# Routing with 112 candidate sums, VectorE in the written order, and placing from an earlier pair on

## The chip, the cores and the metric

The kernel runs on one core of a Trainium2 chip. The metric is the device time of one execution in microseconds (us). Five engines run side by side, each through its own list of instructions in order: TensorE (PE, with its weight loads as PEld), VectorE (DVE), ScalarE (ACT), GpSimd (POOL) and SyncE (SP, which starts the DMAs). An instruction that waits for another engine holds up everything behind it on its own engine.

## The reference, cut to what matters

Two transformer blocks follow each other on 256 tokens of width 1024. The change lies in the feed-forward part at the end of the first block, which looks up single-neuron experts by product keys:

```python
s = jnp.einsum('nhpd,hpkd->nhpk', qry, sub_keys)          # 256 tokens, 8 heads, 2 halves, 128 keys
s_top, i_top = lax.top_k(s, 16)
cand = (s_top[:, :, 0, :, None] + s_top[:, :, 1, None, :]).reshape(n, 8, 16 * 16)
sc, ci = lax.top_k(cand, 16)
e_a = jnp.take_along_axis(i_top[:, :, 0], ci // 16, axis=-1)
e_b = jnp.take_along_axis(i_top[:, :, 1], ci % 16, axis=-1)
experts, gw = e_a * 128 + e_b, jax.nn.softmax(sc, axis=-1)
act = gelu(einsum('td,tkd->tk', xb, u_tab[experts]))       # u_tab, v_tab: 16384 x 1024
out = einsum('tk,tkd->td', gw * act, v_tab[experts])
```

Each token and head takes the 16 best keys of either half, forms 16 x 16 sums of two scores, and keeps the 16 best of these. Since both lists are sorted, the sum of ranks a and b (counted from 0) has at least (a+1)(b+1)-1 sums that are no smaller.

## The kernel before, in words

The kernel does not gather. It multiplies all 16384 rows of `peer_u` with all tokens: 128 blocks of 128 experts, taken two at a time in 64 pairs (`u_pair`, called by `pre`). A pair loads 1 MB of `peer_u` (three buffers, `raw`), which is cut into four pieces of 128x512, called splits here and numbered s0, s1, ... over all pairs, so that pair n has the splits 4n to 4n+3. `split` makes two tiles of each: ACT rounds it to `wh` (L132), and POOL or DVE forms the remainder `wl` (L127); both have four buffers. PE then runs 12 matmuls for each split, 48 for a pair, the third of them being the first that needs `wl`. A gelu on ACT follows (L1074). So the cast of split s has to wait until PE has finished split s-4, whose buffer it takes.

Which engine makes a `wl` goes by a turning pattern, `lo_pat`: while the routing is computed it is `"pppppv"`, five on POOL and the sixth on DVE; while the experts are placed it is `"vp"`.

Routing (`route(t)`, for the two halves t = 0, 1 of the tokens) is DVE work. Per half it runs `top16` (L1110 to L1115) on 16 rows of 128 scores, forms 8 x 256 candidate sums (L1131), runs `top16` on the 8 rows of 256, and turns the found places into expert numbers by comparing, multiplying and adding up over 128x2048 elements (L1149 to L1152, twice). A `top16` is five instructions, each of which needs the one before: the 8 largest (L1111), their places (L1112), their replacement by a very small number (L1113), the next 8 largest (L1114) and their places (L1115). In the profile L1112, L1113 and L1115 are two instructions each, a load of the 8 values (MATCH_VALUE_LOAD) and the search. ACT takes the exponentials of the weights (L1156). PE then transposes the three results `ee` (L1164), and ACT and DVE bring them into `eab` and `gwb` (L1166 to L1172). `route` is a generator: between its pieces the loop calls `pre`, 26 times in all, so the pairs and the routing are written into each other.

Placing follows: for each of 32 groups of eight tokens DVE builds one-hot rows (`onehots`, four instructions of 128x1024), PE multiplies them (L1210, 16 matmuls) and the result, the weights at their experts' places, is multiplied into what `pre` left (`place`). The groups are spread over the pairs from the end of routing up to pair 62.

The order of the instructions on each engine is not the written one: a scheduler sets it when the kernel is built, by its own costs and priorities. It also moves the transposes and the exponential among the pairs.

Of the kernel before, what the change touches and what calls it, by code (L numbers as in the profile page):

```python
# [8 lines left out]
F32 = mybir.dt.float32  # L9
F32R = mybir.dt.float32r  # L10
BF = mybir.dt.bfloat16
HF = mybir.dt.float16
# [7 lines left out]
EPS = 1e-6  # L20
AHEAD = 3
GSC = 16384.0
NEG = -3.0e38
TAKEN = -3.39e38
TAKEN_LIM = -3.2e38
# [29 lines left out]
def block_kernel(ctx, tc, I, out, dbg=None, stop=None):  # L55
# [978 lines left out]
    with ExitStack() as pp:  # L1034
# [42 lines left out]
                V.tensor_tensor(a[:, :, 0:t], pv[:, :, 0:t], a[:, :, 0:t], op=ALU.mult)  # L1077

        npre = 0
        with ExitStack() as pr:  # L1080
            R = pr.enter_context(tc.tile_pool(name="R", bufs=2))
            iota = R.tile([128, 128], F32, name="iota", bufs=1)
# [31 lines left out]
                V.max(vals[:, 8:16], src)  # L1114
                V.max_index(idxs[:, 8:16], vals[:, 8:16], src)  # L1115

            def route(t):
                val = R.tile([128, 16, 16], F32, name="val")
                idx = R.tile([128, 16, 16], U32, name="idx")
                for hp in range(16):  # L1120
                    top16(sc_[t][:, hp * 128:hp * 128 + 128], val[:, hp], idx[:, hp])
                    if hp % 4 == 3:
                        yield
                idf = R.tile([128, 16, 16], HF, name="idf")
                V.tensor_copy(idf, idx)
                cand = z0[:, 4096:6144].rearrange("p (h a b) -> p h a b", h=8, a=16)
                eq = R.tile([128, 8, 16, 16], HF, name="eq", bufs=1)
                vv = val.rearrange("p (h two) k -> p h two k", two=2)
                iv = idf.rearrange("p (h two) k -> p h two k", two=2)
                B4 = [128, 8, 16, 16]  # L1130
                V.tensor_tensor(cand, vv[:, :, 0, :, None].to_broadcast(B4),  # L1131
                                vv[:, :, 1, None, :].to_broadcast(B4), op=ALU.add)
                yield
                top = R.tile([128, 8, 16], F32, name="top")
                ci = R.tile([128, 8, 16], U32, name="ci")
                for hh in range(8):
                    top16(cand[:, hh].rearrange("p a b -> p (a b)"), top[:, hh], ci[:, hh])
                    if hh % 2:
                        yield
                ee = R.tile([128, 3, 128], F32, name="ee")  # L1140
                for w in range(2):
                    cu = R.tile([128, 8, 16], U32, name="cu", bufs=1)
                    if w == 0:
                        V.tensor_single_scalar(cu, ci, 4, op=ALU.logical_shift_right)
                    else:
                        V.tensor_single_scalar(cu, ci, 15, op=ALU.bitwise_and)
                    cf_ = R.tile([128, 8, 16], HF, name="cf", bufs=1)
                    V.tensor_copy(cf_, cu)
                    V.tensor_tensor(eq, cf_[:, :, :, None].to_broadcast(B4),  # L1149
                                    iob[:, None, None].to_broadcast(B4), op=ALU.is_equal)  # L1150
                    V.tensor_tensor(eq, eq, iv[:, :, w, None, :].to_broadcast(B4), op=ALU.mult)
                    V.tensor_reduce(ee[:, w].rearrange("p (h k) -> p h k", h=8), eq, axis=AX.X, op=ALU.add)  # L1152
                    yield
                gw = ee[:, 2].rearrange("p (h k) -> p h k", h=8)
                V.tensor_tensor(gw, top, top[:, :, 0:1].to_broadcast([128, 8, 16]), op=ALU.subtract)
                S.activation(gw, gw, AF.Exp)  # L1156
                gs = R.tile([128, 8], F32, name="gs")
                V.tensor_reduce(gs, gw, axis=AX.X, op=ALU.add)
                V.reciprocal(gs, gs)
                V.tensor_tensor(gw, gw, gs[:, :, None].to_broadcast([128, 8, 16]), op=ALU.mult)  # L1160
                yield
# [5 lines left out]
                gr = R.tile([128, 128], F32, name="gr", bufs=1)  # L1167
                S.mul(gr, q[:, 256:384], GSC)
                for i in range(2):
                    V.tensor_copy(gwb[:, i, ts], gr)  # L1170
                    if i < 1:
                        V.tensor_tensor(gr, gr, gwb[:, i, ts], op=ALU.subtract)  # L1172
                yield

            for g in range(4):
                add(f"pq{g}", I["w_peer_q"][g], "f", pair(xt), qry(g))
            need("pq3")
            lo_pat[0] = "pppppv"
            for t in range(2):
                for _ in route(t):  # L1180
                    pre(npre)
                    npre += 1

        lo_pat[0] = "vp"
        zone["ze"] = Zt("ze").rearrange("p (b t) -> p b t", t=256)
        with ExitStack() as pe:
# [35 lines left out]
            hot = onehots(0)  # L1222
            for n in range(n0, 64):
                pre(n)
                while ng < 32 and ng * (n1 - n0) < 32 * (n + 1 - n0):
# [568 lines left out]
```

## Time and profile before

| | us |
|---|---|
| median of 3 runs (lowest to highest) | 1726.85 (1726.26 to 1728.38) |
| the profiled execution | 1726.9 |
| its span in the profile | 1725.1 |
| PE busy | 1686.9 (98%) |
| DVE busy | 1248.7 (72%) |
| ACT busy | 989.8 (57%) |
| POOL busy | 247.4 (14%) |

The profiled execution stands within 0.1 us of the median of the runs, and 1.8 us of it lie outside the span. The pairs run from about 583 to 1001 us of the span; the routing on DVE lies between 545 and 668 us. The last column but two of a row by stretches of time (PEclk) is the clock granted to PE as a share of its full 2.4 GHz.

### The profile page before, as it was taken

The page shows a single profiled execution, that of the slowest core. Times are in us where ns is not written, and L with a number is a line of the kernel's source. Part 1 is how long each engine was busy: PE and PEld are TensorE (multiplying, and loading weights), DVE is VectorE, ACT ScalarE, POOL GpSimd, SP SyncE. Part 2 cuts the span into 40 slices and gives each one's busy share as a digit, 9 for nine tenths or more (in the row PEclk, how much of TensorE's full clock was granted, in tenths as well). Part 3 has the DMA queues.
Part 4 walks back from the last instruction along what each step waited for, and adds up shares of the span by engine and source line. Part 5 has one row for each costly group of instructions (what it writes and reads, how often), then busy time and mean ns, then how long its engine had stood idle before and what let it go on. Part 6 is the DMA issues. An engine that isn't in the chain of part 4 may idle for free.

```text
span 1725.1 us, 30196 instructions
## 1 busy us (share of the span) xinstructions
PE 1686.9 (98%) x11502; PEld 1523.2 (88%) x11502; DVE 1248.7 (72%) x2517; ACT 989.8 (57%) x1984; POOL 247.4 (14%) x182
## 2 busy tenths in 40 slices
PE   9999999999999988999999999999999899999997
PEld 7988978998989988999999988878888796889996
DVE  7956999557667995066888856656666679688887
ACT  7565687556555544555555555545555663666664
POOL 0000000000000477754444400000000000000001
PEclk9999999999999999999999999999999999999998
DMA  6448424555445444544445465575555547345552
GB/s 249 157 165 291 171 91 137 191 199 186 151 142 202 160 147 147 195 171 149 167 151 172 147 205 192 193 281 194 193 194 195 210 172 306 128 177 196 175 193 98
DMA packets 45746, 312.22 MB, mean 181 GB/s; under 512 B 5536, under 2 KB 6048, under 8 KB 8992
## 3 DMA queue, kind: packets, MB, share of 16 engines
q1 hardware_dynamic: 45600, 310.29, 51.5%
q8 instruction: 90, 1.47, 0.3%
q14 instruction: 56, 0.46, 0.1%
HBM read 307.65 MB, written 2.62 MB: 180 GB/s over the span
## 4 chain that ended last, share of the span: by engine, by line
PE 90%; DVE 6%; ACT 2%; DMA 1%; issue 1%; POOL 1%; SPq 0%; POOLq 0%; ACTq 0%
PE y L1258 7%; PE y L1257 7%; PE pm L1065 7%; PE y L1259 7%; PE pm L1067 6%; PE pm L1066 6%; PE pm L204 6%; PE pm L206 6%; PE pm L205 6%; PE pm L197 4%; PE pm L198 4%; PE pm L196 4%; PE pt L204 2%; PE pt L206 2%; PE pt L205 2%; PE pt L1210 2%
## 5 line engine op out<-in xcount | busy, mean ns | idle before, releaser
L132 ACT CAST wh<-raw 128x512 fp32r<-128x512 f32 (+1 forms) x1048 | 643.7, 621 | 555.1 <-PE pm L1066 172.6
L127 DVE TENSOR_TENSOR wl<-raw,wh 128x512 fp32r<-128x512 f32 (+1 forms) x886 | 607.6, 692 | 328.1 <-ACT wh L132 326.1
L1067 PE MATMUL pm<-xhi,wl 128*128 128x256 f32 x1024 | 292.3, 285 | 8.4 <-POOL wl L127 4.9
L1065 PE MATMUL pm<-xhi,wh 128*128 128x256 f32 x1024 | 294.4, 288 | 0.0
L1066 PE MATMUL pm<-xlo,wh 128*128 128x256 f32 x1024 | 291.6, 285 | 0.0
L127 POOL TENSOR_TENSOR wl<-raw,wh 128x512 fp32r<-128x512 f32 x162 | 229.9, 1423 | 250.9 <-ACT wh L132 246.8
L1067 PEld LDWEIGHTS pm<-xhi,wl 128*128 128x128 f32 x1024 | 198.2, 194 | 9.7 <-POOL wl L127 5.5
L1066 PEld LDWEIGHTS pm<-xlo,wh 128*128 128x128 f32 x1024 | 198.6, 194 | 0.0
L1065 PEld LDWEIGHTS pm<-xhi,wh 128*128 128x128 f32 x1024 | 198.1, 193 | 0.0
L204 PE MATMUL pm<-xhi,wh 128*128 128x256 f32 x640 | 182.6, 286 | 1.0 <-ACT wh L132 1.0
L206 PE MATMUL pm<-xhi,wl 128*128 128x256 f32 x640 | 180.9, 284 | 1.0 <-DVE wl L127 1.0
L205 PE MATMUL pm<-xlo,wh 128*128 128x256 f32 x640 | 181.1, 283 | 0.5 <-DVE xlo L309 0.5
L204 PEld LDWEIGHTS pm<-xhi,wh 128*128 128x128 f32 x640 | 122.4, 192 | 6.0 <-issue 3.4
L206 PEld LDWEIGHTS pm<-xhi,wl 128*128 128x128 f32 x640 | 122.3, 192 | 2.3 <-DVE wl L127 1.4
L205 PEld LDWEIGHTS pm<-xlo,wh 128*128 128x128 f32 x640 | 122.6, 192 | 1.7 <-issue 0.8
L204 PE MATMUL pt<-xhi,wh 128*128 128x256 f32 x320 | 90.9, 284 | 0.0
L206 PE MATMUL pt<-xhi,wl 128*128 128x256 f32 x320 | 90.5, 283 | 0.0
L205 PE MATMUL pt<-xlo,wh 128*128 128x256 f32 x320 | 90.5, 283 | 0.0
L197 PE MATMUL pm<-wl,xhi 128*128 128x512 f32 (+1 forms) x192 | 76.1, 396 | 0.1
L196 PE MATMUL pm<-wh,xhi 128*128 128x512 f32 (+1 forms) x192 | 74.7, 403 | 1.4 <-ACT wh L132 1.2
L198 PE MATMUL pm<-wh,xlo 128*128 128x512 f32 (+1 forms) x192 | 74.4, 390 | 0.0
L204 PEld LDWEIGHTS pt<-xhi,wh 128*128 128x128 f32 x320 | 61.3, 192 | 0.9 <-ACT ua L1628 0.4
(1057 smaller groups left out, 3576.2 us busy)
## 6 DMA issues: line engine op xcount, KB each, us to landing
raw<-peer_u SPq DMA_DIRECT2D x64, 1024.0 KB, 4.8
raw<-peer_v SPq DMA_DIRECT2D x64, 1024.0 KB, 4.8
raw<-w_in SPq DMA_DIRECT2D x54, 1024.0 KB, 4.9
raw<-w_up SPq DMA_DIRECT2D x22, 1024.0 KB, 4.9
raw<-w_ada SPq DMA_DIRECT2D x21, 1024.0 KB, 5.3
raw<-w_down SPq DMA_DIRECT2D x11, 1024.0 KB, 4.8
raw<-w_cross_kv SPq DMA_DIRECT2D x8, 1024.0 KB, 4.8
raw<-w_ssd_branch SPq DMA_DIRECT2D x8, 1024.0 KB, 5.0
```

The costliest lines, as they stand in the source:

```text
L127: (V if e == "v" else G).tensor_sub(o, a, b)
L132: S.copy(wh, src)
L196: PE.matmul(pb[t], hi[:, ts], wh, start=first, stop=False)
L197: PE.matmul(pb[t], hi[:, ts], wl, start=False, stop=False)
L198: PE.matmul(pb[t], lo[:, ts], wh, start=False, stop=last)
L204: PE.matmul(o, wh[:, ns], hi, start=first and b % 2 == 0, stop=False)
L205: PE.matmul(o, wh[:, ns], lo, start=False, stop=False)
L206: PE.matmul(o, wl[:, ns], hi, start=False, stop=last and b % 2 == 1)
L1065: PE.matmul(o, wh[:, k % 4], hi[:, k], start=k == 0 and i == 0, stop=False)
L1066: PE.matmul(o, wh[:, k % 4], lo[:, k], start=False, stop=False)
L1067: PE.matmul(o, wl[:, k % 4], hi[:, k], start=False, stop=k == 7 and i == 1)
L1257: PE.matmul(o, ah_[:, ts], vh, start=False, stop=False)
```

## The change

The diff has four parts. The candidate sums become 112: ranks 0 to 3 of the first half with all 16 of the second, and ranks 4 to 15 with the first 4. The place c of a candidate then stands for rank pair (c // 16, c % 16) below 64 and ((c - 48) // 4, c % 4) from there on; the first key's number is found by adding up differences (`dl`) over all ranks whose `start` is not above c, the second by comparing a masked place `bm` with 0 to 15. DVE keeps the written order from the loop's beginning to its end (`manual_schedule`). `route` gives a cost with each piece, and a pair is written whenever the costs have added up to 4.8. The transposes and what follows them are a generator of their own (`turn`), which is continued at later pairs. During routing DVE makes every fifth `wl` instead of every sixth (`"ppppv"`).

```diff
+ROUTE_STEP = 4.8
...
+        gr = [X1P.tile([128, 128], F32, name=f"gr{t}") for t in range(2)]
+        late_turn = deque()
...
+            NC = 112
+            start = R.tile([128, 16], HF, name="start", bufs=1)
+            V.tensor_scalar(start, iota[:, 0:16], 4.0, 48.0, op0=ALU.mult, op1=ALU.add)
+            V.scalar_tensor_tensor(start, iota[:, 0:16], 16.0, start, op0=ALU.mult, op1=ALU.min)
-            def route(t):
+            def route(t, out):
...
                     top16(sc_[t][:, hp * 128:hp * 128 + 128], val[:, hp], idx[:, hp])
-                    if hp % 4 == 3:
-                        yield
+                    yield 1.17
+                cand = z0[:, 4096:4096 + 8 * NC].rearrange("p (h c) -> p h c", h=8)
...
+                for o, a, n in ((0, 0, 16), (64, 4, 4)):
+                    w = 4 if a == 0 else 12
+                    V.tensor_tensor(cand[:, :, o:o + w * n].rearrange("p h (a b) -> p h a b", b=n),
+                                    vv[:, :, 0, a:a + w, None].to_broadcast([128, 8, w, n]),
+                                    vv[:, :, 1, None, 0:n].to_broadcast([128, 8, w, n]), op=ALU.add)
...
-                V.tensor_tensor(cand, vv[:, :, 0, :, None].to_broadcast(B4),
-                                vv[:, :, 1, None, :].to_broadcast(B4), op=ALU.add)
-                yield
+                dl = R.tile([128, 8, 16], HF, name="dl", bufs=1)
+                V.tensor_copy(dl[:, :, 0:1], iv[:, :, 0, 0:1])
+                V.tensor_tensor(dl[:, :, 1:16], iv[:, :, 0, 1:16], iv[:, :, 0, 0:15], op=ALU.subtract)
+                yield 2.0
...
                 for hh in range(8):
-                    top16(cand[:, hh].rearrange("p a b -> p (a b)"), top[:, hh], ci[:, hh])
-                    if hh % 2:
-                        yield
+                    top16(cand[:, hh], top[:, hh], ci[:, hh])
+                    yield 1.1
...
-                    V.tensor_tensor(eq, cf_[:, :, :, None].to_broadcast(B4),
-                                    iob[:, None, None].to_broadcast(B4), op=ALU.is_equal)
-                    V.tensor_tensor(eq, eq, iv[:, :, w, None, :].to_broadcast(B4), op=ALU.mult)
-                    V.tensor_reduce(ee[:, w].rearrange("p (h k) -> p h k", h=8), eq, axis=AX.X, op=ALU.add)
-                    yield
+                V.tensor_tensor(eq, ci[:, :, :, None].to_broadcast(B4),
+                                start[:, None, None].to_broadcast(B4), op=ALU.is_ge)
+                yield 2.2
+                V.tensor_tensor(eq, eq, dl[:, :, None, :].to_broadcast(B4), op=ALU.mult)
+                yield 1.7
+                V.tensor_reduce(ee[:, 0].rearrange("p (h k) -> p h k", h=8), eq, axis=AX.X, op=ALU.add)
+                bm = R.tile([128, 8, 16], U32, name="bm", bufs=1)
+                V.tensor_scalar(bm, ci, 64.0, 12.0, op0=ALU.is_ge, op1=ALU.mult)
+                V.tensor_single_scalar(bm, bm, 15, op=ALU.bitwise_xor)
+                V.tensor_tensor(bm, bm, ci, op=ALU.bitwise_and)
...
-            lo_pat[0] = "pppppv"
-            for t in range(2):
-                for _ in route(t):
-                    pre(npre)
-                    npre += 1
+            lo_pat[0] = "ppppv"
+            debt = 0.0
+            with tc.manual_schedule(engines={mybir.EngineType.DVE}):
+                for t in range(2):
+                    got = []
+                    for cost in route(t, got):
+                        debt += cost
+                        if debt >= ROUTE_STEP:
+                            debt -= ROUTE_STEP
+                            pre(npre)
+                            npre += 1
+                            if late_turn and next(late_turn[0], 0) == 0:
+                                late_turn.popleft()
+                    late_turn.append(turn(t, got[0]))
+                pre(npre)
+                npre += 1
+                next(late_turn[-1])
```

What this does to the order shows on DVE. Line numbers of the changed kernel are larger, by one at `split` and by three in `top16`. Before, right behind the `wl` of split s1, the searches stand two by two in each other:

```order
L127 TENSOR_TENSOR wl<-raw,wh 128x512
L1113 MATCH_REPLACE zr<-val,zr 128x128
L1111 MAX val<-zr 128x8
L1114 MAX val<-zr 128x8
L1112 MAX_INDEX idx<-val,zr 128x8
L1115 MAX_INDEX idx<-val,zr 128x8
L1113 MATCH_REPLACE zr<-val,zr 128x128
L1114 MAX val<-zr 128x8
L1115 MAX_INDEX idx<-val,zr 128x8
L1111 MAX val<-zr 128x8 x2
L1112 MAX_INDEX idx<-val,zr 128x8 x2
L1113 MATCH_REPLACE zr<-val,zr 128x128 x2
```

Now, at the same place, one search stands behind the other:

```order
L1117 MAX val<-zr 128x8
L1118 MAX_INDEX idx<-val,zr 128x8
L128 TENSOR_TENSOR wl<-raw,wh 128x512
L1114 MAX val<-zr 128x8
L1115 MAX_INDEX idx<-val,zr 128x8
L1116 MATCH_REPLACE zr<-val,zr 128x128
L1117 MAX val<-zr 128x8
L1118 MAX_INDEX idx<-val,zr 128x8
```

Before, an instruction of another search stood between most pairs that depend on each other; now each of the five stands right behind the one it needs. Of the 32 searches of 128 scores 5 stand ahead of s1 now, and 22 before, where the scheduler had put them among the query products ahead of the pairs.

The second place is the end of the second half on DVE, from the last sum over `eq` to the first one-hot rows (`oa`, `ob`). Before:

```order
L1152 TENSOR_REDUCE ee<-eq 128x128
L127 TENSOR_TENSOR wl<-raw,wh 128x512
L1160 TENSOR_TENSOR ee<-ee,gs 128x128
L1170 CAST gwb<-gr 128x128
L1172 TENSOR_TENSOR gr<-gr,gwb 128x128
L1170 CAST gwb<-gr 128x128
L127 TENSOR_TENSOR wl<-raw,wh 128x512 x9
L1170 CAST gwb<-gr 128x128
L1172 TENSOR_TENSOR gr<-gr,gwb 128x128
L1170 CAST gwb<-gr 128x128
L1198 TENSOR_TENSOR oa<-io_6044,eab 128x1024
```

Now:

```order
L1174 TENSOR_REDUCE ee<-eq 128x128
L1176 TENSOR_REDUCE gs<-ee 128x8
L1177 RECIPROCAL gs<-gs 128x8
L1178 TENSOR_TENSOR ee<-ee,gs 128x128
L128 TENSOR_TENSOR wl<-raw,wh 128x512 x3
L1231 TENSOR_TENSOR oa<-io_6044,eab 128x1024
L1232 TENSOR_TENSOR ob<-io_6044,eab 128x1024
L1191 CAST gwb<-gr_6046 128x128
L1233 TENSOR_TENSOR ob<-ob,gwb 128x1024
L1193 TENSOR_TENSOR gr_6046<-gr_6046,gwb 128x128
L1234 TENSOR_TENSOR ob<-ob,gwb 128x1024
```

Nine `wl` lay between the end of routing and the casts of the second half, and now three lie ahead of the first one-hot rows. On PE the first group of `place` stood behind 27 pairs and now stands behind 19; the three transposes of the first half stand behind pair 9 (one behind 4.8 pairs and two behind 12 before), and those of the second half behind 15.3 (one) and 18 (two) pairs (25 before). DVE's `wl` are now the splits s1, s6, s11 and so on to s71; between s51 and s56 stand all eight searches of the candidate sums of the second half.

## Rows read from the trace of the kernel before

**Rows 1.** The page's span and its part 1: busy time of each engine.
```profile
span 1725.1 us, 30196 instructions
...
PE 1686.9 (98%) x11502; PEld 1523.2 (88%) x11502; DVE 1248.7 (72%) x2517; ACT 989.8 (57%) x1984; POOL 247.4 (14%) x182
```
**Rows 2.** Stretches: length, busy PE, PEld, DVE, ACT, POOL, PEclk, DMA share, GB/s.
```profile
600.00:620.00 20.00, 13.78 (x100) 12.87 (x98) 20.00 (x52) 8.57 (x14) 13.25 (x9) 0.91 0.28 100
...
640.00:660.00 20.00, 16.66 (x135) 16.06 (x133) 19.86 (x59) 11.12 (x18) 15.24 (x11) 1.00 0.37 125
660.00:680.00 20.00, 18.55 (x142) 18.55 (x143) 10.88 (x13) 8.76 (x16) 12.36 (x10) 0.91 0.56 186
```
**Rows 3.** The chain that ended last, in order of time: start, length, what.
```profile
744.89 0.33 PE pt L1164 x3
...
797.23 0.94 PE pt L1210 x16
...
803.97 0.94 PE pt L1210 x16
...
816.46 0.94 PE pt L1210 x16
```
**Rows 4.** PE in order of time, 602 to 615 us: start, length; idle before it.
```profile
602.31 0.28 PE L1066 MATMUL pm<-xlo,wh 128*128 128x256 f32 x1
603.48 0.39 PE L1067 MATMUL pm<-xhi,wl 128*128 128x256 f32 x1 [0.89 <-DVE wl L127]
...
613.64 0.39 PE L1067 MATMUL pm<-xhi,wl 128*128 128x256 f32 x1 [2.69 <-POOL wl L127]
...
614.65 0.41 PE L1066 MATMUL pm<-xlo,wh 128*128 128x256 f32 x1
614.86 0.41 PE L1067 MATMUL pm<-xhi,wl 128*128 128x256 f32 x1
```
**Rows 5.** DVE in order of time, searches of the first half.
```profile
585.18 0.27 DVE L1113 MATCH_REPLACE8 zr<-val,zr 128x128 f32<-128x128 f32 x1
585.49 0.29 DVE L1114 MAX8 val<-zr 128x8 f32<-128x128 f32 x1
585.81 0.09 DVE L1115 MATCH_VALUE_LOAD idx<-val,zr 128x8 f32 x1
585.89 0.29 DVE L1115 FIND_INDEX8 idx<-val,zr 128x8 uint32<-128x128 f32 x1
586.10 0.47 DVE L1111 MAX8 val<-zr 128x8 f32<-128x128 f32 x2
...
588.43 0.46 DVE L1111 MAX8 val<-zr 128x8 f32<-128x128 f32 x2
```
**Rows 6.** Line 1111 on 256 values: shortest, median, longest in ns, first and last start.
```profile
L1111 DVE MAX8 top<-zr x16: 400/404/419, 593.8 to 649.1; 128x8 f32<-128x256 f32 x16
```
**Rows 7.** The tile eq: shortest, median, longest in ns.
```profile
L1149 DVE TENSOR_TENSOR eq<-cf,iob x4: 2270/2278/2291, 610.2 to 661.3; 128x2048 f16<-128x2048 f16 x4
L1151 DVE TENSOR_TENSOR eq<-eq,idf x4: 1207/1209/2312, 613.6 to 663.7; 128x2048 f16<-128x2048 f16 x4
L1152 DVE TENSOR_REDUCE ee<-eq x4: 2273/2278/2284, 617.0 to 665.0; 128x128 f32<-128x2048 f16 x4
```
**Rows 8.** DVE and POOL in order of time: a small operation twice, a wl.
```profile
609.45 0.22 DVE L1144 TENSOR_SCALAR cu<-ci 128x128 uint32<-128x128 uint32 x1
...
612.38 1.29 DVE L1146 TENSOR_SCALAR cu<-ci 128x128 uint32<-128x128 uint32 x1
...
619.24 0.68 DVE L127 TENSOR_TENSOR wl<-raw,wh 128x512 fp32r<-128x512 f32 x1
619.84 2.28 DVE L1149 TENSOR_TENSOR eq<-cf,iob 128x2048 f16<-128x2048 f16 x1
...
610.47 7.79 POOL L127 TENSOR_TENSOR wl<-raw,wh 128x512 fp32r<-128x512 f32 x4 [3.63 <-ACT wh L132]
```

**Rows 9.** The page's part 5: busy us, mean ns; idle before it and its releaser.
```profile
L132 ACT CAST wh<-raw 128x512 fp32r<-128x512 f32 (+1 forms) x1048 | 643.7, 621 | 555.1 <-PE pm L1066 172.6
```

More of the change, by code (lines that the diff above doesn't have):

```diff
@@ L1115, in top16 @@
                 V.max_index(idxs[:, 8:16], vals[:, 8:16], src)
-            def route(t):
+            NC = 112
+            start = R.tile([128, 16], HF, name="start", bufs=1)
+            V.tensor_scalar(start, iota[:, 0:16], 4.0, 48.0, op0=ALU.mult, op1=ALU.add)
+            V.scalar_tensor_tensor(start, iota[:, 0:16], 16.0, start, op0=ALU.mult, op1=ALU.min)
+            B4 = [128, 8, 16, 16]
+            def route(t, out):
                 val = R.tile([128, 16, 16], F32, name="val")
@@ L1121, in route @@
                     top16(sc_[t][:, hp * 128:hp * 128 + 128], val[:, hp], idx[:, hp])
-                    if hp % 4 == 3:
-                        yield
+                    yield 1.17
+                cand = z0[:, 4096:4096 + 8 * NC].rearrange("p (h c) -> p h c", h=8)
+                eq = R.tile([128, 8, 16, 16], HF, name="eq", bufs=1)
+                vv = val.rearrange("p (h two) k -> p h two k", two=2)
+                for o, a, n in ((0, 0, 16), (64, 4, 4)):
[3 more added lines that the diff above has]
+                                    vv[:, :, 1, None, 0:n].to_broadcast([128, 8, w, n]), op=ALU.add)
                 idf = R.tile([128, 16, 16], HF, name="idf")
                 V.tensor_copy(idf, idx)
-                cand = z0[:, 4096:6144].rearrange("p (h a b) -> p h a b", h=8, a=16)
-                eq = R.tile([128, 8, 16, 16], HF, name="eq", bufs=1)
-                vv = val.rearrange("p (h two) k -> p h two k", two=2)
                 iv = idf.rearrange("p (h two) k -> p h two k", two=2)
-                B4 = [128, 8, 16, 16]
-                V.tensor_tensor(cand, vv[:, :, 0, :, None].to_broadcast(B4),
-                                vv[:, :, 1, None, :].to_broadcast(B4), op=ALU.add)
-                yield
+                dl = R.tile([128, 8, 16], HF, name="dl", bufs=1)
+                V.tensor_copy(dl[:, :, 0:1], iv[:, :, 0, 0:1])
+                V.tensor_tensor(dl[:, :, 1:16], iv[:, :, 0, 1:16], iv[:, :, 0, 0:15], op=ALU.subtract)
+                yield 2.0
                 top = R.tile([128, 8, 16], F32, name="top")
@@ L1136, in route @@
                 for hh in range(8):
-                    top16(cand[:, hh].rearrange("p a b -> p (a b)"), top[:, hh], ci[:, hh])
-                    if hh % 2:
-                        yield
+                    top16(cand[:, hh], top[:, hh], ci[:, hh])
+                    yield 1.1
                 ee = R.tile([128, 3, 128], F32, name="ee")
[L1141 to L1148, printed above, removed]
-                    V.tensor_tensor(eq, cf_[:, :, :, None].to_broadcast(B4),
-                                    iob[:, None, None].to_broadcast(B4), op=ALU.is_equal)
-                    V.tensor_tensor(eq, eq, iv[:, :, w, None, :].to_broadcast(B4), op=ALU.mult)
-                    V.tensor_reduce(ee[:, w].rearrange("p (h k) -> p h k", h=8), eq, axis=AX.X, op=ALU.add)
-                    yield
+                V.tensor_tensor(eq, ci[:, :, :, None].to_broadcast(B4),
[8 more added lines that the diff above has]
+                V.tensor_tensor(bm, bm, ci, op=ALU.bitwise_and)
                 gw = ee[:, 2].rearrange("p (h k) -> p h k", h=8)
@@ L1156, in route @@
                 S.activation(gw, gw, AF.Exp)
+                yield 2.9
+                V.tensor_tensor(eq, bm[:, :, :, None].to_broadcast(B4),
+                                iob[:, None, None].to_broadcast(B4), op=ALU.is_equal)
+                yield 2.2
+                V.tensor_tensor(eq, eq, iv[:, :, 1, None, :].to_broadcast(B4), op=ALU.mult)
+                yield 1.7
+                V.tensor_reduce(ee[:, 1].rearrange("p (h k) -> p h k", h=8), eq, axis=AX.X, op=ALU.add)
                 gs = R.tile([128, 8], F32, name="gs")
@@ L1160, in route, with turn @@
                 V.tensor_tensor(gw, gw, gs[:, :, None].to_broadcast([128, 8, 16]), op=ALU.mult)
-                yield
+                out.append(ee)
+                yield 2.7
+            def turn(t, ee):
                 q = PT()
@@ L1166, in route @@
                 S.copy(eab[:, :, ts], q[:, 0:256].rearrange("p (w t) -> p w t", w=2))
-                gr = R.tile([128, 128], F32, name="gr", bufs=1)
-                S.mul(gr, q[:, 256:384], GSC)
+                S.mul(gr[t], q[:, 256:384], GSC)
+                yield
                 for i in range(2):
-                    V.tensor_copy(gwb[:, i, ts], gr)
+                    V.tensor_copy(gwb[:, i, ts], gr[t])
                     if i < 1:
-                        V.tensor_tensor(gr, gr, gwb[:, i, ts], op=ALU.subtract)
+                        V.tensor_tensor(gr[t], gr[t], gwb[:, i, ts], op=ALU.subtract)
                 yield
@@ L1224, in block_kernel @@
                 pre(n)
+                while late_turn:
+                    if next(late_turn[0], 0) == 0:
+                        late_turn.popleft()
                 while ng < 32 and ng * (n1 - n0) < 32 * (n + 1 - n0):
```

## Prediction

> **What bounds the kernel now.** I read the page's busy times first. PE is busy for 1686.9 of 1725.1 us [rows 1], so a change on DVE can only gain where PE waits. The stretches show where: in 600 to 620, 640 to 660 and 660 to 680 us PE is busy for 13.78, 16.66 and 18.55 of 20 us [rows 2], 11.0 us of idle time together, while DVE is busy almost throughout. PE in order of time shows what it waits for: a `wl`, made by DVE itself or by POOL behind an ACT that waits for the routing [rows 4]. The granted clock is 0.91 in two of these stretches [rows 2]: behind a wait two matmuls start 0.21 us apart [rows 4], about half speed (1.2 of 2.4 GHz).
>
> The chain of waits gives the pace without disturbance. A pair and a placing group take 803.97 - 797.23 = 6.74 us, two pairs and a group 816.46 - 803.97 = 12.49 us [rows 3], so a pair takes 5.75 us (taken as 5.76: 48 matmuls of 0.12 us, 1.44 us a split). The matmul at 602.31 us stands 3.25 pairs and one matmul behind the first [rows 4], so the pairs began at about 583.5 us. Pair 25 should follow at 583.5 + 25 x 5.76 + 0.4 for the first three transposes = 727.9 us. The transposes that stand ahead of it start at 744.89 us [rows 3]. So routing costs PE 17.0 us: about 13 us of waiting, and 4 us for some 43 matmuls that run 0.09 us longer each. That is all the change can win; while placing, the pace of rows 3 has no wait in it, and fewer groups per pair win nothing there.
>
> **The change: what a search costs.** In the old order two searches in each other take 588.43 - 586.10 = 2.33 us, 1.17 us each [rows 5]. In the new order each instruction stands right behind the one that it needs. The only such places before are at the ends of runs: from MATCH_REPLACE8 to the MAX8 that reads its result 0.31 us, from this MAX8 to the load behind it 0.32 us, where an independent MAX8 follows 0.21 us behind FIND_INDEX8 [rows 5]. So a dependent instruction starts when the one before has ended. Adding up one search: 0.32 (MAX8 to load), 0.08 to FIND_INDEX8, 0.21 to 0.32 to the next load, 0.07, 0.31, 0.32, 0.08, 0.21 = 1.60 to 1.71 us; the uncertain step is one of the trace of before does not show. I take 1.66 us. MAX8 takes 404 ns on 256 values [rows 6] and 0.28 to 0.29 us on 128 [rows 5], 1 ns per value, so a search of 112 is 5 x 16 ns cheaper: 1.58 us.
>
> The Trainium skill's "VectorE: DVE Perf Modes", section "The DRAIN you can't avoid", says that a semaphore behind each VectorE instruction costs nothing extra, since the next one waits for an empty pipeline anyway. Rows 5 differ (0.21 against 0.31 us), and by the rule the outcome would be the first rival below.
>
> **Other work.** The comparisons and the sums over 2048 elements stay at 2.2 us, the products at 1.15 us: their medians [rows 7] less the 0.07 us or so by which the next one starts before the end (a `wl` lasts 0.68 us, and 0.60 us lie to the next start) [rows 8]. Between these come three small operations on `bm` and one on the weights, nearest to the 0.22 us of row 609.45 with 0.04 us of waiting [rows 8]; I take 1.05 us for the four, so comparison, product, sum and these are 6.65 us. The 896 candidate sums, by their share of a 2048-element operation about 1.0 us, with the cast and `dl` come to 1.85 us. They replace 2.2 us. A `wl` costs DVE these 0.60 us.
>
> **Where it lies.** Before, 22 of the 32 searches of 128 were done while PE worked on the query products, now 5 are; 27 stand among the pairs. DVE's fixed list can now be laid against PE's 7.2 us from one `wl` of DVE to the next (five splits). The cast of split s waits for split s-4, so a `wl` can be ready at most 3 x 1.44 - 0.62 - 0.68 + 0.24 = about 3.2 us ahead (ACT's cast takes 0.62 us [rows 9], the `wl` 0.68, and PE runs two matmuls before it needs it). DVE against PE, from `wl` to `wl`:
> s1 to s11, twice four searches: 7.24 us each, ahead throughout.
> s11 to s16: 3 x 1.66 + 1.85 + 3 x 1.58 + 0.6 = 12.2 us, 5.0 too many, less 3.2 ahead: PE waits 1.8.
> s16 to s21: 5 x 1.58 + 0.6 = 8.5: waits 1.3. s21 to s26: 6.65 + 0.6: 0.05. s26 to s31: 2.8, ahead again by 3.2.
> s31 to s36: 1.15 + 2.2 + 0.8 + 5 x 1.66 + 0.6 = 13.05 against 7.6 with the transposes: waits 2.2.
> s36 to s41: 0.85 for the three small operations on `gr` at 0.28 each, 4 x 1.66 + 0.6 = 8.1: 0.9. s41 to s46: 0. s46 to s51: 7.4: 0.2.
> s51 to s56: all eight candidate searches, 8 x 1.58 + 0.6 = 13.2: waits 6.0. s56 to s61: 0, then ahead.
> Together 12.5 us. The exponentials on ACT stand behind s28 and s63, where their input is there in time, and the transposes behind 15.3 and 18 pairs find theirs too.
>
> **Two additions.** A small operation takes 1.29 instead of 0.22 us at 612.38 us, while POOL makes a `wl` [rows 8]; in the routing of before eight instructions of DVE lost 0.8 to 1.1 us so (the product with 2312 instead of 1207 ns in rows 7 is another). The changed list has about ten such chances, of which some six lie where DVE is late: 0 to 6.5 us. I take 3, half, because POOL runs out of splits when PE stands. The Trainium skill's "SBUF — State Buffer", section "Who interferes with whom", says that the instruction of VectorE or GpSimd that starts first holds the pair of ports to its end and the other waits; by that rule the loss is up to one whole POOL instruction, and the trace agrees with 1.07 us. Second, the clock: the 43 slow matmuls of before cost 4 us; of the new waits only the one of 6 us surely resembles those, and a slow PE gives a late DVE time to catch up. 0 to 4 us, taken as 1.5.
>
> **The sum.** Gone: 17.0. New: 12.5 + 3 + 1.5 = 17.0 us. The profiled execution took 1726.9 us, its span 1725.1, and stands 0.1 us above the median: 1726.9 - 17.0 + 17.0 = 1726.9. The bounds of this case: with the search at 1.60 instead of 1.66 (0.06 us at some 30 searches that lie in late stretches, 1.8 us), no port loss and no slow clock 1726.9 - 17.0 + 10.7 = 1720.6; with 1.71 (1.5 more), 5 of the port and 2 of the clock 1726.9 - 17.0 + 21.0 = 1730.9. My forecast: no change that a measurement of this kernel can tell (0.2%, 3.5 us, is about its limit).
>
> **The rivals.** First, the dependent steps cost no more than now, and a search is 1.17 us (1.09 at 112). For it speaks that this is what rows 5 show on average, against it the single steps of the same rows. Then s11 to s16 takes 9.2 us and s51 to s56 9.3 us, both within the 3.2 us ahead; only s31 to s36 (10.6 against 7.6) comes near. PE waits under 1.5 us: 1726.9 - 17.0 + 1.0 = 1711.
> Second, slower: the block of DVE behind POOL. It decides once more than about five of the ten chances are hit in late stretches, since each then moves PE by 1.07 us and each wait keeps the clock low for the splits behind it. With all 6.5 us and 3.5 us of slow matmuls: 1726.9 - 17.0 + 12.5 + 10 = 1732.4, and 1734 with the search at 1.71. For it: PE stands four times or more in the list above. Against it: POOL makes four of five splits instead of five of six, and stands when PE stands.
> Third, the first placing group: it stood behind 27 pairs and stands behind 19 now. By the list PE comes to s61 at 583.5 + 61 x 1.44 + 12.5 = 683.8 us, and DVE ends the routing 7 us later, at 691. It then waits for s74, whose cast needs PE to have ended s70 (698 us), until about 700, and has four one-hot operations and the casts of the second half ready between 703 and 706; PE asks for them behind 19 pairs, at 706. A blocked instruction more makes PE wait 1 to 3 us: up to 1730.
>
> **How the numbers follow.** No change as worked out 0.5, the first rival 0.2, the second 0.22, the third 0.08. Of the forecast's own range, 1720.6 to 1730.9, a quarter lies below 1723.4 and a tenth above 1730.3. Faster by over 0.2%: 0.2 + 0.5 x 0.25 + 0.02 = 0.35; slower: 0.22 + 0.5 x 0.1 + 0.02 = 0.29; within: 0.36. The range that should hold the time 8 times in 10 takes in the first rival and reaches to the second's end: 1710 to 1734.
>
> **What would show it.** In the profile after, MAX8 on 112 or 128 values followed by its own load at 0.32 us confirms the price of a search, 0.20 us refutes it and gives the first rival. PE idle shows between s51 and s56 (about 670 to 677 us) for some 6 us, and shorter before s16, s21 and s36, each ended by a DVE `wl`. If PE is idle for under 3 us in all between 583 and 700 us, the sum is wrong by its largest term; if over 16, the port or the clock has decided. If the first transposes are what PE waits for, the list's assumption about them is wrong.

## The result and the profile after

The changed kernel takes 1736.4 us (median of 4 runs, 1735.0 to 1737.5) against 1727.1 us for the kernel before (4 runs beside it): ratio 1.0053, 95% interval 1.004 to 1.0065. It is slower by some 9 us; the forecast was no change, with a range up to 1734, so it lies above the range. The profiled execution took 1735.0 us. By the prediction's count 1709.9 us (1726.9 - 17.0) are left without any cost of routing, so routing now costs PE 25.1 instead of 17.0 us.

The page of the kernel after, its span and part 1, against [rows 1]:

```profile
span 1733.2 us, 30230 instructions
...
PE 1689.6 (97%) x11502; PEld 1525.0 (88%) x11502; DVE 1268.1 (73%) x2538; ACT 992.8 (57%) x2000; POOL 229.0 (13%) x169
```

DVE is busy for longer although each of its 16 searches of sums (eight for each half) is shorter. The stretches of the kernel after, with the columns of [rows 2], show where PE loses time:

```profile
600.00:620.00 20.00, 16.12 (x120) 15.71 (x120) 18.72 (x82) 7.79 (x14) 11.03 (x10) 0.91 0.36 129
620.00:640.00 20.00, 18.06 (x150) 17.86 (x150) 18.31 (x20) 11.60 (x18) 15.16 (x10) 1.00 0.48 159
640.00:660.00 20.00, 15.72 (x119) 15.51 (x118) 18.49 (x89) 7.07 (x14) 10.40 (x9) 0.91 0.36 116
660.00:680.00 20.00, 17.06 (x130) 16.86 (x130) 18.83 (x75) 8.27 (x14) 11.93 (x9) 0.91 0.46 157
680.00:700.00 20.00, 15.35 (x111) 15.14 (x110) 19.13 (x49) 7.96 (x13) 9.94 (x6) 0.83 0.26 97
```

PE falls short in all five of these stretches; before it was three [rows 2]. In order of time PE stands seven times, once for POOL (0.30 us at 701.15) and six times for a `wl` of DVE (start, length; in brackets the idle time before):

```profile
609.93 0.39 PE L1068 MATMUL pm<-xhi,wl 128*128 128x256 f32 x1 [2.99 <-DVE wl L128]
...
619.75 0.39 PE L1068 MATMUL pm<-xhi,wl 128*128 128x256 f32 x1 [0.89 <-DVE wl L128]
...
629.15 0.39 PE L1068 MATMUL pm<-xhi,wl 128*128 128x256 f32 x1 [1.94 <-DVE wl L128]
...
648.40 0.39 PE L1068 MATMUL pm<-xhi,wl 128*128 128x256 f32 x1 [4.28 <-DVE wl L128]
...
674.68 0.39 PE L1068 MATMUL pm<-xhi,wl 128*128 128x256 f32 x1 [2.94 <-DVE wl L128]
...
688.26 0.58 PE L1068 MATMUL pm<-xhi,wl 128*128 128x256 f32 x1 [4.65 <-DVE wl L128]
```

These are splits 16, 21, 26, 36, 51 and 56; with POOL's, 18.0 us of waiting. Mostly behind the four longest waits, 67 matmuls start 0.21 instead of 0.12 us apart (15 of them from 611.38 to 614.59 us), 6.3 us. Counted the same way the kernel before shows 11.0 us of waits and 4.0 us of slow matmuls. So 9.3 us are new. The two profiled executions lie 8.1 us apart and the medians 9.3, so these two kinds of loss make up the whole difference, to within about 1 us.

DVE in the kernel after, in order of time: one search of 128, then the instructions that took longer than the same ones elsewhere, to the end of the sums in the second half; last two rows of POOL.

```profile
579.97 0.29 DVE L1114 MAX8 val<-zr 128x8 f32<-128x128 f32 x1
580.29 0.09 DVE L1115 MATCH_VALUE_LOAD idx<-val,zr 128x8 f32 x1
580.37 0.28 DVE L1115 FIND_INDEX8 idx<-val,zr 128x8 uint32<-128x128 f32 x1
580.69 0.09 DVE L1116 MATCH_VALUE_LOAD zr<-val,zr 128x8 f32 x1
...
581.69 0.28 DVE L1114 MAX8 val<-zr 128x8 f32<-128x128 f32 x1
...
601.92 1.95 DVE L1139 TENSOR_TENSOR zr<-val 128x512 f32<-128x512 f32 x2
...
617.93 1.77 DVE L128 TENSOR_TENSOR wl<-raw,wh 128x512 fp32r<-128x512 f32 x1
619.62 3.37 DVE L1155 TENSOR_TENSOR eq<-ci,start 128x2048 f16<-128x2048 uint32 x1
623.02 2.21 DVE L1158 TENSOR_TENSOR eq<-eq,dl 128x2048 f16<-128x2048 f16 x1
...
632.67 1.58 DVE L128 TENSOR_TENSOR wl<-raw,wh 128x512 fp32r<-128x512 f32 x1 [1.38 <-ACT wh L133]
...
638.16 1.04 DVE L1178 TENSOR_TENSOR ee<-ee,gs 128x128 f32<-128x128 f32 x1
...
655.82 0.92 DVE L128 TENSOR_TENSOR wl<-raw,wh 128x512 fp32r<-128x512 f32 x1
...
669.22 2.25 DVE L1139 TENSOR_TENSOR zr<-val 128x512 f32<-128x512 f32 x2
671.39 1.35 DVE L1143 CAST idf<-idx 128x256 f16<-128x256 uint32 x1
672.78 1.12 DVE L1146 COPY dl<-idf 128x8 f16<-128x8 f16 x1
673.81 0.22 DVE L1147 TENSOR_TENSOR dl<-idf 128x120 f16<-128x120 f16 x1
673.95 0.68 DVE L128 TENSOR_TENSOR wl<-raw,wh 128x512 fp32r<-128x512 f32 x1
...
651.09 1.28 POOL L128 TENSOR_TENSOR wl<-raw,wh 128x512 fp32r<-128x512 f32 x1 [5.60 <-ACT wh L133]
...
669.28 4.58 POOL L128 TENSOR_TENSOR wl<-raw,wh 128x512 fp32r<-128x512 f32 x3 [1.45 <-ACT wh L133]
```

MAX8 to its own load takes 0.32 us and the search 581.69 - 579.97 = 1.72 us: the upper end of the price foreseen (1.60 to 1.71). The second part was foreseen only as a small term: while POOL makes three `wl`, a copy of eight numbers a row takes 1.12 us and a cast 1.35.

### The profile page after: what moved, and what is told of

Read it like the earlier page. It is cut to its first block, busy times and chain, and to the rows that moved or that the text cites. A ratio compares the mean times of both kernels' runs of the same rounds, so it can differ in the third digit from the quotient of the medians.

```text
span 1733.2 us, 30230 instructions
## 1 busy us (share of the span) xinstructions
PE 1689.6 (97%) x11502; PEld 1525.0 (88%) x11502; DVE 1268.1 (73%) x2538; ACT 992.8 (57%) x2000; POOL 229.0 (13%) x169
## 4 chain that ended last, share of the span: by engine, by line
PE 57%; DVE 4%; ACT 1%; POOL 1%; issue 1%; POOLq 0%; ACTq 0%
PE y L1293 7%; PE y L1295 7%; PE y L1294 7%; PE pm L1068 6%; PE pm L1066 6%; PE pm L1067 5%; PE pt L205 2%; PE pt L207 2%; PE pt L206 2%; PE pt L1243 2%; PE pm L199 1%; PE pm L197 1%; PE pm L198 1%; PE dn L1701 1%; PE dn L1703 1%; PE dn L1702 1%
## 5 line engine op out<-in xcount | busy, mean ns | idle before, releaser
L128 DVE TENSOR_TENSOR wl<-raw,wh 128x512 fp32r<-128x512 f32 (+1 forms) x899 | 621.1, 698 | 303.5 <-ACT wh L133 301.4
L1068 PE MATMUL pm<-xhi,wl 128*128 128x256 f32 x1024 | 293.9, 287 | 18.1 <-DVE wl L128 17.7
L128 POOL TENSOR_TENSOR wl<-raw,wh 128x512 fp32r<-128x512 f32 x149 | 211.5, 1424 | 279.2 <-ACT wh L133 276.7
```

What stands on the lines that cost most here:

```text
L128: (V if e == "v" else G).tensor_sub(o, a, b)
L1068: PE.matmul(o, wl[:, k % 4], hi[:, k], start=False, stop=k == 7 and i == 1)
```

## The experiments

All ran beside the kernel before, whose medians were 1726.8, 1727.0 and 1727.7 us. "Waits" and "slow" are counted in each trace as above. Added to the 1709.9 us without any cost of routing, waits and slow matmuls leave up to 4.1 us of a profiled execution unexplained, so this count alone does not settle differences of a few us. The medians of the kernel before differ by 0.9 us, so a difference between two versions that did not run side by side can be off by as much. The counts of 19 and 27 pairs in these texts are the pairs ahead of the first placing group; one fewer, 18 and 26, is written among the routing. The 23 pairs at a step of 4.0 are likewise 22 among the routing.

| version | median us | ratio to before (95%) | waits + slow, us |
|---|---|---|---|
| changed kernel | 1736.4 | 1.004 to 1.0065 | 18.0 + 6.3 |
| searches two by two | 1724.0 | 0.9971 to 0.9990 | 9.1 + 2.6 |
| scheduler's order | 1730.2 | 1.0007 to 1.0027 | 15.1 + 2.6 |
| step 3.4 | 1722.3 | 0.9964 to 0.9984 | 7.7 + 0.3 |
| every wl on POOL | 1728.7 | 1.0003 to 1.0023 | 12.9 + 3.6 |
| without POOL's wl | 1725.9 | 0.9984 to 1.0003 | 11.5 + 4.4 |
| idle matmuls, first | 1738.5 | 1.0047 to 1.0081 | 8.6 + 1.3 |
| idle matmuls, half | 1738.2 | 1.0049 to 1.0083 | 13.3 + 2.5 |
| 112 sums alone | 1723.1 | 0.9968 to 0.9987 | 8.9 + 1.4 |
| scheduler's order, one of six | 1725.4 | 0.9982 to 1.0001 | 9.3 + 2.5 |
| two by two, step 4.0 | 1714.7 | 0.9911 to 0.9944 | 3.3 + 1.7 |
| two by two, true costs | 1714.6 | 0.9909 to 0.9942 | 3.4 + 0.3 |

**The blocks by POOL.**

```diff
-            lo_pat[0] = "ppppv"
+            lo_pat[0] = "oooov"     # o: no wl is made; PE reads one fixed tile
```

> The changed kernel in which the four of five wl that POOL makes in the routed stretch are left out: PE multiplies with one fixed tile of zeros in their place (these products lack their low part). VectorE keeps its list word for word, its dependent searches and its own wl of every fifth split; only POOL stands still, so that nothing can block VectorE. Theory 1 (blocks by POOL are a large part of the waits: eight instructions of VectorE ahead of s56 lost some 9 us in the changed kernel's trace): the sums, the cast, the copy and the products show 0.3 to 1.2 us each without a 1.07 us surplus, the waits before s26 and s51 go, those before s16, s36 and s56 stay at about 2, 2.5 and 4 us: 9 us instead of 18.0, with 3 us of slow clock 12 instead of 24.3: 1723 us. Theory 2 (the price of the searches alone makes the waits): 16 us of waits stay with 5 or 6 of slow clock, 1733 us.

Measured 1725.9 us, 10.5 less than the changed kernel and nearer to theory 1 (1723) than to theory 2 (1733); the waits fell by 6.5 us. Those before s21, s26 and s51 are gone, the last two as theory 1 says; s16, s36 and s56 have 2.47, 2.78 and 6.21 us. The last is longer than in the changed kernel (4.65 us), not about 4 us as expected. The difference is near the 1.4 us that the 15 slow matmuls behind the wait before s51 gave DVE there. DVE of this kernel in order of time, the same place as above:

```profile
663.76 1.14 DVE L1145 TENSOR_TENSOR zr<-val 128x512 f32<-128x512 f32 x2
664.82 0.29 DVE L1149 CAST idf<-idx 128x256 f16<-128x256 uint32 x1
665.14 0.19 DVE L1152 COPY dl<-idf 128x8 f16<-128x8 f16 x1
665.23 0.22 DVE L1153 TENSOR_TENSOR dl<-idf 128x120 f16<-128x120 f16 x1
665.37 0.68 DVE L129 TENSOR_TENSOR wl<-raw,wh 128x512 fp32r<-128x512 f32 x1
```

The same list, 1.14, 0.29 and 0.19 instead of 2.25, 1.35 and 1.12 us. Over the whole run, shortest, median and longest in ns, no comparison and no product is long any more; those for the first key:

```profile
L1161 DVE TENSOR_TENSOR eq<-ci,start x2: 2284/2286/2287, 618.1 to 679.5; 128x2048 f16<-128x2048 uint32 x2
...
L1164 DVE TENSOR_TENSOR eq<-eq,dl x2: 1224/1224/1225, 620.5 to 681.9; 128x2048 f16<-128x2048 f16 x2
```

**The clock.** Idle matmuls on PE ahead of the splits where it waits longest; `keep_clock(n)` issues n products of the identity with itself.

```diff
+FILL = {16: 16, 36: 24, 51: 16, 56: 28}     # in the second kernel 8, 12, 8, 14
...
                     if k % 4 == 0:
+                        keep_clock(FILL.get(4 * bp + 2 * i + k // 4, 0))
```

> The changed kernel with 16, 24, 16 and 28 idle matmuls (128 columns, 0.126 us each by an earlier row of such ones, 10.6 us in all) on PE ahead of splits 16, 36, 51 and 56, where it waited 2.99, 4.28, 2.94 and 4.65 us, each filling some 1 us less than the wait. VectorE's work is the same. Theory 1 (the slow clock behind a wait is an extra cost of its own): the waits shrink by what is filled, the clock stays up, and 4 to 5 of the 6.3 us of slow matmuls come back: 1731.5 us. Theory 2 (VectorE is late anyhow, and a slow PE only gives it the time that PE would wait for later): the later waits grow by what the clock gives, 1735 to 1737 us.

Measured 1738.5 us: nothing won, but the trace showed my filling to be twice what I had meant, so it decides nothing. The second:

> The kernel with idle matmuls again, but 8, 12, 8 and 14 of them: in the trace of the first one each took two passes, 0.23 us instead of 0.126 (32 records in 3.73 us for 16 matmuls), so that 19 us were filled where 14.9 us of waits stood. Now it is 9.7 us, 1 to 1.4 us less than each wait. Theory 1 (the slow clock is an extra cost): 4 to 5 us come back against the changed kernel, 1731.5 us, the clock stays up and the four waits show 1 to 1.5 us each. Theory 2 (a slow PE only uses time that it would wait for VectorE): the later waits grow by as much, 1735 to 1737 us.

Measured 1738.2 us. PE in order of time, three of the four fillings (L189) and waits behind them:

```profile
607.63 1.95 PE L189 MATMUL pt<-ident 128*128 128x128 f32 x16
...
611.02 0.39 PE L1070 MATMUL pm<-xhi,wl 128*128 128x256 f32 x1 [1.21 <-DVE wl L129]
...
620.75 0.39 PE L1070 MATMUL pm<-xhi,wl 128*128 128x256 f32 x1 [2.28 <-DVE wl L129]
...
644.27 2.84 PE L189 MATMUL pt<-ident 128*128 128x128 f32 x24
...
649.49 0.39 PE L1070 MATMUL pm<-xhi,wl 128*128 128x256 f32 x1 [2.14 <-DVE wl L129]
...
657.84 0.39 PE L1070 MATMUL pm<-xhi,wl 128*128 128x256 f32 x1 [0.89 <-DVE wl L129]
...
666.16 0.39 PE L1070 MATMUL pm<-xhi,wl 128*128 128x256 f32 x1 [0.87 <-DVE wl L129]
...
683.68 3.29 PE L189 MATMUL pt<-ident 128*128 128x128 f32 x28
...
690.21 0.58 PE L1070 MATMUL pm<-xhi,wl 128*128 128x256 f32 x1 [3.01 <-DVE wl L129]
```

Behind the first filling no matmul is slow, and the next wait (s21) is 2.28 instead of 0.89 us. Behind the second PE waits before s41 and s46, 0.89 and 0.87 us, where it did not wait in the changed kernel, and before s56 filling and wait together are 6.3 instead of 4.65 us. In all 10.0 us are filled, 13.3 waited, 2.5 slow: 25.8 us, against 18.0 + 6.3 = 24.3. Slow matmuls went from 6.3 to 2.5 us and no time came back. Theory 2 holds, though the time lies 1 us above its range: a slow PE spends time that it would otherwise wait for DVE. The number of the slow matmuls is not to be added to DVE's lateness.

**The searches.**

```diff
-    for hp in range(16):
-        top16(sc_[t][:, hp * 128:hp * 128 + 128], val[:, hp], idx[:, hp])
-        yield 1.17
+    for hp in range(0, 16, 2):
+        top16x2(...)      # each of the five steps for hp, then for hp + 1
+        yield 2.34        # the searches of sums likewise
```

> The changed kernel with its top-16 searches written two by two: the same five steps, each for search A and then for search B, so that no step stands right behind the one it needs; nothing else changes (the split points of VectorE stay within one search of where they were). Theory 1 (the dependent steps of the written order are what makes PE wait): a search costs 1.17 us on 128 and about 1.09 us on 112 values instead of the 1.71 and 1.62 us of the changed kernel's trace. VectorE from split s11 to s16 then takes about 9.9 us and from s51 to s56 9.3 us, both within the lead; PE waits some 3 us before s36 and hardly elsewhere, 3 us in all instead of 18.0, with 1.5 us of slow clock instead of 6.3: 1735.0 - 24.3 + 4.5 = 1715 us, faster than the kernel before. Theory 2 (the large operations and their blocking by POOL decide): the waits before s26, s36 and s51 stay, 8 to 10 us with the slow clock behind them, and the time is 1725 to 1730 us.

Measured 1724.0 us, 12.4 less than the changed kernel but 9 more than theory 1 gave, just under theory 2's range. DVE of this kernel in order of time, first steps of two pairs of searches that follow each other:

```profile
589.44 0.48 DVE L1122 MAX8 val<-zr 128x8 f32<-128x128 f32 x2
...
591.79 0.46 DVE L1122 MAX8 val<-zr 128x8 f32<-128x128 f32 x2
```

That is 2.35 us for two, the 1.17 us each of the order before, so the dependent steps do cost 0.54 us a search. What stayed is in part theory 2's: both products of line 1170 take 2.20 us here, against 1.22 without POOL's `wl`, and PE waits 3.6 us for POOL beside 5.5 us for DVE (before s16 and s36). The theories are not rivals; each holds for a part. Line 1170 over the whole run, shortest, median and longest in ns:

```profile
L1170 DVE TENSOR_TENSOR eq<-eq,dl x2: 2202/2204/2207, 616.6 to 677.3; 128x2048 f16<-128x2048 f16 x2
```

**The step between pairs.**

```diff
-ROUTE_STEP = 4.8
+ROUTE_STEP = 3.4
```

> The changed kernel with a step of 3.4 instead of 4.8 us between pairs, so that 27 pairs instead of 19 stand among the routing and each has about three searches of VectorE beside it instead of four or five. The searches keep their dependent steps. Theory 1 (VectorE is given more work per pair than a pair lasts, because the written costs of 1.17 and 1.1 us are 0.53 us too low): with 3 searches an interval takes 5.7 of PE's 7.2 us; PE waits only where a search interval and the sums or the decoding meet, about 0.5 us before s16, 2.3 before s36 and 1.6 before s76, with 1.5 us of slow clock 6 us instead of 24.3: 1717 us. Theory 2 (waits come from the blocking of the large operations, wherever they stand): 10 us of waits and slow clock at least, 1722 to 1730 us. If placing behind 27 pairs instead of 19 costs something, it shows as a longer time with no wait between 583 and 740 us.

Measured 1722.3 us, 14.1 less than the changed kernel. The time lies in theory 2's range, but waits and slow clock, 8.0 us, lie between the 6 of theory 1 and the 10 of theory 2. No step of a search was changed; the routing only has 26 pairs to be done beside instead of 18.

**Every wl on POOL.**

```diff
-            lo_pat[0] = "ppppv"
+            lo_pat[0] = "p"
```

> The changed kernel with every wl of the routed stretch on POOL instead of four of five: VectorE does nothing there that PE waits for but the transposes' input. Theory 1 (PE waits for VectorE's own wl behind the searches): all six waits for VectorE go; POOL needs 1.29 to 1.44 us a split against PE's 1.44 and falls behind only while large operations block it, some 8 us, with 4 us of slow clock 12 instead of 24.3 us: 1723 us. Theory 2 (the port: POOL blocked by VectorE's large operations and the other way round costs as much as the order): POOL at the 1.98 us a split that the five splits from 695 us show is behind for most of the stretch, and PE waits over 18 us for POOL: 1730 us or more.

Measured 1728.7 us, between the theories, and by a way that neither had. PE does not wait for a `wl` of DVE, but its longest wait, 7.28 us, is for a cast of ACT. ACT of this kernel in order of time:

```profile
678.01 1.28 ACT L1167 ACT_TABLE_LOAD   x1
689.07 0.31 ACT L1167 ACTIVATE ee<-ee 128x128 f32<-128x128 f32 x1 [9.78 <-DVE ee L1166]
689.28 2.16 ACT L133 CAST wh<-raw 128x512 fp32r<-128x512 f32 x4
```

The exponential waits 9.78 us for DVE, and the casts stand behind it. So here a late DVE still holds PE, through the next thing that it feeds.

**The order and the sums.**

```diff
-            with tc.manual_schedule(engines={mybir.EngineType.DVE}):
+            with ExitStack():
```

> The changed kernel without the written order on VectorE: the scheduler orders VectorE as in the kernel before, so that 22 of the 32 searches of 128 stand ahead of the first pair again and searches stand in one another; 112 sums, the new decoding and the 19 pairs stay. Theory 1 (the order is what costs): routing ends behind split 41 instead of 71, VectorE falls behind PE's 7.2 us by 2.7, 1.6, 1.1, 0.8, 1.1 and 2.3 us in the intervals from s6 to s36, 9.6 us less a lead of 3.2, so PE waits 6.4 us, with 3 us of port and 3 us of slow clock 12.4 instead of 17.0 us: 1722 us, faster than before. Theory 2 (the new candidate sums and decoding are dearer than the old): no gain over before, 1727 to 1733 us.

Measured 1730.2 us, in theory 2's range: the written order costs 6.2 us at this spacing, but the gain over the kernel before that theory 1 expected did not come. Two more kernels ask why. The first is the kernel before with L1131 and L1143 to L1152 replaced by the new sums and decoding, and nothing else:

> The kernel before with the 112 sums and their decoding alone: the scheduler orders VectorE, 27 pairs, POOL's five of six wl and the places of the pairs stay as before. Theory 1 (fewer sums are a gain by themselves, some 11 us of VectorE's search time less, which the written order then loses again): intervals of six splits (8.64 us) exceed by 2.4, 2, 1 and 3.3 us, less a lead of 3.2, so some 5.5 us of waits, 3 of port and 1.5 of slow clock instead of 15.0: 1720 us. Theory 2 (the sums and the decoding give more chances to be blocked than they save, as the free order with 19 pairs at 1730 us suggests): 1726 to 1730 us.

Measured 1723.1 us, faster than before by 0.13 to 0.32%: the sums are a gain by themselves, though a smaller one than theory 1's 1720 us, and theory 2 falls. The second changes the pattern in the kernel with the scheduler's order:

```diff
-            lo_pat[0] = "ppppv"
+            lo_pat[0] = "pppppv"
```

> The changed kernel without the written order (1730 us) and with VectorE making one wl of six instead of one of five, as in the kernel before; 19 pairs and the rest stay. The step between pairs does not alter VectorE's list under the scheduler, so that the two kernels of this order, 1723.1 us (sums alone, one of six, 27 pairs) and 1730.2 us (one of five, 19 pairs), differ by the split pattern and by where placing begins. Theory 1 (the pattern: with one of five PE waits for VectorE eight times instead of six while the routing lasts): 1723 to 1725 us. Theory 2 (placing behind 19 pairs instead of 27 costs something): 1728 to 1731 us, with waits of 9 us as in the sums alone.

Measured 1725.4 us. So one `wl` of five instead of six on DVE costs 4.8 us in this order: PE waits for DVE seven times (14.6 us) with the one pattern, four times (7.3 us) with the other. The 2.3 us that are left to the sums alone may be the 19 pairs; since the scheduler's list also differs in places, that stays open.

In a row these versions take the change apart: the sums alone -3.9 us (against 1727.0 beside them), 19 pairs with the later transposes +2.3, one `wl` of five on DVE +4.8, the written order +6.2, together the 9.4 us from 1727.0 to 1736.4. The steps were added in this sequence only; a pattern of one in six in the written order was not run.

**Two versions that beat both.** Two by two with `ROUTE_STEP = 4.0`:

> The changed kernel with the searches written two by two and a step of 4.0 instead of 4.8 us between pairs (23 pairs beside the routing). Both causes of a late VectorE are smaller: by the prices of the traces no interval of five splits exceeds PE's 7.2 us by more than the 3.2 us of lead. Theory 1: waits of 2 to 3 us, next to no slow clock: 1714 us, faster than all so far. Theory 2 (what is left is POOL's wl behind VectorE's large operations, 3.6 us in the two-by-two kernel, which a smaller step doesn't change): 1718 to 1721 us.

Measured 1714.7 us, theory 1's. Then with the costs as measured:

```diff
-ROUTE_STEP = 4.0
+ROUTE_STEP = 4.2
...
-                yield 2.0      # sums, cast, dl; likewise 1.7 -> 2.2, 2.9 -> 3.4, 2.7 -> 3.5
+                yield 3.4
```

> The two-by-two kernel with the costs of the routing's steps written as the traces show them, blocks by POOL included (sums, cast and dl 3.4, products 2.2, the sum with what follows it 3.4 and 3.5 us instead of 2.0, 1.7, 2.9 and 2.7) and a step of 4.2 us. The pairs then stand evenly by VectorE's true time. Theory 1 (what is left in the version of step 4.0 is one interval too full, the 2.2 us before s76 and the slow clock behind it): 1712 us. Theory 2 (the rest is POOL behind VectorE's large operations and the spread between runs): 1714 to 1716 us.

Measured 1714.6 us (1714.0 to 1715.5), theory 2's: against the kernel before 0.6 to 0.9% faster, and no different from the version of step 4.0. What PE still waits for in it (us in total, times, longest):

```profile
PE pm L1068 <- POOL wl L128: 2.5, 3, 1.1
PE pm L1068 <- DVE wl L128: 0.9, 1, 0.9
```

## Why the prediction was wrong

**What held.** PE was the bound, and the price of a search in written order was 1.66 foreseen and 1.72 measured (112 values: 1.58 and 604.33 to 605.97, 1.64). The ledger from `wl` to `wl` (the section "Where it lies") held too. By the rows of DVE the interval s11 to s16 took 13.14 us (12.2 foreseen), s16 to s21 8.72 (8.5), s21 to s26 10.47 (7.25), s31 to s36 15.01 (13.05), s36 to s41 8.14 (8.1), s46 to s51 10.45 (7.4), s51 to s56 13.58 (13.2). Four are off by 0.9 us or more, and each holds instructions that are longer than in the kernel without POOL's `wl`. Between s21 and s26 the `wl` at 617.93, the comparison and the product lose 1.09, 1.08 and 0.99 us; without them 7.3 us are left. Between s46 and s51 the sums, cast and copy lose 1.11, 1.06 and 0.93 us, which leaves 7.35 us. Between s31 and s36 the `wl` at 632.67 (1.58 us) and the product of the weights (1.04 instead of 0.29 us) lose 1.65, which leaves 13.4 us. From s11 to s16 it is 0.93, most of it at the sums of 601.92, which leaves 12.2 us. So the list that I wrote down from the rows of before was right to within half a microsecond wherever POOL did not meddle. The kernel without POOL's `wl` is that list run by itself: its waits are 11.5 us, all before s16, s36 and s56, where 12.5 were foreseen.

**What failed** is the step "Two additions". Its first term, blocks by POOL, was "0 to 6.5 us. I take 3, half, because POOL runs out of splits when PE stands". The count of ten chances was right; what was taken off it, first to six and then by half, was not. Ten instructions of DVE ahead of s56 (601.92, 617.93, 619.62, 623.02, 632.67, 638.16, 655.82, 669.22, 671.39 and 672.78 us above) lost 9.0 us together, and taking POOL's work away gave 10.5 us back.

POOL does run out of splits in most of the stands: PE stands from 644.12 to 648.40 us, and POOL, done by 645.49, is idle until 651.09 us. But that saves little, since six of the ten blocked instructions run wholly while PE still works and POOL has splits, and add to DVE's lateness at the next stand. Before s51 not even the reason held: PE stands from 671.74 to 674.68 us, and POOL works from 669.28 to 673.86 us on three `wl` of the next splits (ACT's last cast for them starts at 671.48 us), while the cast and the copy of DVE lose 1.06 and 0.93 us. With the 9.0 us counted in place of 3 the sum is 1732.9 us, with the 10.5 us measured 1734.4 us; the profiled execution took 1735.0.

The second term, 1.5 us for the clock, measured 6.3 us, but it was wrong in kind: the kernel with idle matmuls shows that slow matmuls lie within DVE's lateness, and that removing them wins nothing.

Two readings of the kernel before were off without deciding the outcome. DVE is busy in only 10.88 of the 20 us from 660 on [rows 2], not almost throughout. And of the 17.0 us of routing the trace shows 11.0 us of waits, not about 13, of which 2.60 us were not for a `wl` but for DVE's input to the first transpose:

```profile
619.38 0.33 PE L1164 MATMUL pt<-ident,ee 128*128 128x128 f32 x1 [2.60 <-DVE ee L1152]
```

**The rivals.** The second was what happened: blocks by POOL, decided by more than five of ten chances hit. It was given 0.22 and 1734 us at most, with a price of 6.5 us that left out that the new sums, cast and copy stand together ahead of one `wl`. The Trainium skill's "SBUF — State Buffer", section "Who interferes with whom", names instructions of VectorE with two inputs in SBUF as those that contend with GpSimd, copies and casts as those that can, and reductions as free of it. The trace agrees: sums, products, a comparison, `wl`, cast and copy lost up to 1.1 us each, and the reductions over `eq` (2.29 us at either time) nothing.
The first rival, 1711 us by searches of 1.17 us, did not come, because the price was what the single steps of [rows 5] said; even with that price restored by another order the time is 1724.0 us, since the blocks remain. The rule in the Trainium skill's "VectorE: DVE Perf Modes", section "The DRAIN you can't avoid", by which a semaphore between two instructions costs nothing, does not hold for this chain: 1.72 us a search with each step behind the one it needs, 1.17 us with one other step between.
The third, the first placing group, shows no wait: PE stands for 0.10 us between 720 and 724 us.

**The list of what would show it** named the right place: with over 16 us of idle PE between 583 and 700 us "the port or the clock has decided". It was 17.7 us. The clock as a cost of its own is excluded by the idle matmuls; that blocks by POOL are the larger part of what was missing is shown by the kernel without its `wl`.

## What to carry to other kernels

When one engine's fixed list feeds another at a fixed pace, write the list from one handover to the next and price each entry; that worked here. Then count, entry by entry, which of them a neighbour can block, and put each down at the full price of one block; a discount for times at which the neighbour should be idle needs a row that shows it idle at that entry. An order written by hand must also do what a scheduler did unasked: put another instruction between two that depend on each other, and leave room enough from one handover to the next. The two together, with 22 pairs among the routing instead of 18, turned 1736.4 into 1714.7 us; writing the other costs as measured added nothing that can be told apart (1714.6 us).

## What was not expected of the hardware

Three changes that each look like a repair of their own, searches two by two (12.4 us), 26 pairs instead of 18 among the routing (14.1 us) and a silent POOL (10.5 us), won 37 us one by one, where only 25.1 us were to be had: they all make the same DVE less late, and cannot be added. And the clock of PE, 1.2 instead of 2.4 GHz by the spacing of the matmuls (0.21 instead of 0.12 us) behind each of the four longest waits, cost nothing of its own while DVE was the one that was late.
